# First-layer attention heads in pairs, and weights stored in runs of 4096 bytes

## The chip, the cores and the metric

The kernel runs on one core of a Trainium2 chip. The metric is the device time of one execution in microseconds, the median of several. The engines are called PE (matmul), PEld (PE's weight load), DVE (VectorE), ACT (ScalarE), POOL (GpSimd) and SP (SyncE, which issues nearly all DMAs here).

## The reference

Two blocks of two layers each work on 256 tokens of width 1024, in float32.

- The first block's layer, run twice: RMS norm with a modulation computed from a vector c; one projection into queries, keys and values of two attentions and two gates; attention A with 8 query heads on 2 key heads, a sliding window of 128 and a learned sink per head; attention B with 8 heads, which for 256 tokens is plain causal attention; two output projections, gated and added; `w_out`; then an MLP of width 4096 with squared ReLU.
- The second block: a pooling mixer and a mixture of 16 experts of width 256 (its layer 0, for 512 tokens: latent and context), then attention of 16 heads over latent and context and a second mixture of experts (its layer 1, 256 tokens). Each token goes to two experts of one group.

```
s = einsum('bnqhgd,bnkhd->bnhgqk', qb, kb) * HEAD_DIM ** -0.5     # masked, HEAD_DIM = 64
p = softmax(concatenate([s, sink], axis=-1), axis=-1)[..., :-1]   # attention A; B has no sink
hid = silu(h @ w_gate) * (h @ w_up) * gates;  y = hid @ w_down    # an expert
```

## The kernel before, in words

**Weights.** `plan` writes out one list of all weight pieces in the order in which they are used: pieces of 512 KB, 128 partitions by 1024 floats. `feed` has SP load the next piece of the list into a raw buffer as soon as one is free (7 raw buffers and, at stages, some pages of a shared pool). `pump` splits a piece into a high part H (a cast on ACT, L309) and a rest L (a subtraction on DVE, L310); `take` hands H and L to PE, which multiplies three times with them (L149 to L151). Between the weights stand pieces of the modulation matrices `w_ada` and `w_mod_2`, which DVE adds up (L353).

A weight matrix lies in memory as rows. A piece of `w_in`, `w_up`, `w_out`, `w_down`, `w_o_*` or `attn_wqkv_2` is 2 rows of 512 columns for each partition, so its DMA reads runs of 2048 bytes. A gate and up piece of an expert comes from two matrices with rows of 256 floats, so it takes two DMAs with runs of 1024 bytes. The pieces of `w_ada`, `w_mod_2` and of the experts' down matrix `moe_wd_2` already have runs of 4096 bytes.

**Order.** The program is written in Python in the order of the algorithm; a planner then orders the instructions of each engine by priority and by its own estimate of when each is ready, and gives out the buffers. An engine runs its list in that order and waits in place.

**Projection.** `block1` runs the first block's layer. Its in-projection has nine column blocks c; `proj` does a block in 8 parts (4 pieces times 2 token tiles), a part being 6 matmuls of 512 columns. After each part `fill` counts a tick and emits the work that `later` put down for that tick. The attention units are put down so: those of attention A after block 2, at ticks 2, 4, ..., 20, those of attention B after block 4, at ticks 2, 5, ..., 29.

**Attention units.** `attn_units` makes 10 units for 8 heads; unit i does S(i), T(i-1) and O(i-2).

- S (L917 to L938), one head: a matmul that puts the mask into a bank of PSUM, the scores of the first 128 queries against 128 keys and of the second 128 against 256, with contraction over 64 partitions (the even heads lie in partitions 0 to 63, the odd ones in 64 to 127); two maxima, the product with the scale, the minimum with the sink, two exponentials with their sums, the sink's exponential, the reciprocal, and two products with it.
- T (L945, L947): three transposes of 128x128 and a copy.
- O (L957 to L959): three products with the values, whose 64 result rows go to the lower or upper half of a bank; after the second head of a pair the result is split (L962, L963).

A float32 matmul is two instructions on PE, a transpose is one. `acc` gives one of 4 PSUM banks, `sm` (the probabilities) has 2 buffers, `pT` has 2.

**Experts.** In the second block's layer 0 an expert gathers 96 token rows from memory (POOL's indirect DMA, L1387), transposes and splits them (L1399 to L1402), multiplies (`gate_up`), takes silu (L1283), multiplies with the down matrix and adds the rows back to memory by an indirect DMA (L1440). In layer 1 the rows are gathered and scattered by matmuls. `attention2` (L1583 to L1616) already has its heads in pairs for O: the matmuls of two heads alternate between the lower and the upper 64 result rows. `dense_rest` runs only where an expert has over 96 tokens.

Of the kernel before, what the change touches and what calls it, by code (L numbers as in the profile page):

```python
# [12 lines left out]
F32 = mybir.dt.float32  # L13
# [5 lines left out]
AF = mybir.ActivationFunctionType  # L19
ALU = mybir.AluOpType  # L20
# [4 lines left out]
P = 128  # L25
# [58 lines left out]
class Kern:  # L84
# [75 lines left out]
    def plan(s):  # L160
# [14 lines left out]
        def kn(ap):  # L175
            return ap.rearrange("(k p) n -> p k n", p=P)
# [21 lines left out]
        def cols(key, src, c0, w0=512):  # L198
            for q in range(2):
                w(key + (q,), [(None, kn(src[q * 512:(q + 1) * 512, c0:c0 + w0]))], [P, 4, 512])  # L200

        def halves(key, src):
            for h in range(2):
                w(key + (h,), [(None, kn(src[:, h * 512:(h + 1) * 512]))], [P, 4, 512])

        s.rate = 0.0
        for l in range(2):
            if f"b1{l}" not in S:
                continue
            need(l, 1)  # L210
            s.rate = RATES[l][0]
            cols(("in", l, 0), A["w_in"][l], 0)
            w(("in", l, 1, 0), [(None, kn(A["w_in"][l][:, 512:768]))], [P, 8, 256])
            for i in range(7):
                cols(("in", l, 2 + i), A["w_in"][l], 768 + 512 * i)
            need(l, 2)
            halves(("oa", l), A["w_o_swa"][l])
            halves(("ob", l), A["w_o_moba"][l])
            for h in range(2):
                cols(("out", l, h), A["w_out"][l], 512 * h)  # L220
            need(l, 4)
            s.rate = RATES[l][1]
            for i in range(8):
                cols(("up", l, i), A["w_up"][l], 512 * i)
                if i == 6:
                    need(l, 5)
                if i:
                    halves(("dn", l, i - 1), A["w_down"][l][512 * (i - 1):512 * i])
            halves(("dn", l, 7), A["w_down"][l][512 * 7:])

        s.rate = 0.0

        def moe(l):
            for e in range(16):
                for q in range(2):
                    w(("gu", l, e, q),
                      [(0, kn(A["moe_wg_2"][l, e][q * 512:(q + 1) * 512])),
                       (1, kn(A["moe_wu_2"][l, e][q * 512:(q + 1) * 512]))], [P, 4, 512])
                if e:
                    w(("wd", l, e - 1), [(None, kn(A["moe_wd_2"][l, e - 1]))], [P, 2, 1024])  # L240
            w(("wd", l, 15), [(None, kn(A["moe_wd_2"][l, 15]))], [P, 2, 1024])
# [7 lines left out]
        if "l1" in S:  # L249
            need(3, 1)  # L250
            s.rate = RATES[2]
            for i in (2, 0, 1):
                s.rate = RATES[2] if i < 2 else 0
                cols(("qkv", i), A["attn_wqkv_2"][0], 512 * i)
            s.rate = 0.0
            need(3, 5)
            for i in range(2):
                halves(("wo", i), A["attn_wo_2"][0][512 * i:512 * (i + 1)])
            moe(1)
# [393 lines left out]
    def block1(s, l):  # L653
# [253 lines left out]
    def attn_units(s, l, br, qT, kT, v, oH, oL, qs):  # L907
        nc = s.nc
        pts, sms, ops = {}, {}, {}

        def S(h):
            b = (h % 2) * 64
            kp = (0 if (h // 4) == (h % 2) else 1) if br == 0 else 2 + h // 2
            q = qT[b:b + 64, 4 * br + h // 2]
            k = kT[b:b + 64, kp]
            ps = s.acc()
            nc.tensor.matmul(ps[:, 0:384], s.identb, s.maskb[br], start=True, stop=False, skip_group_check=True)  # L917
            nc.tensor.matmul(ps[:, 0:128], q[:, 0:128], k[:, 0:128], start=False, stop=False, skip_group_check=True)
            nc.tensor.matmul(ps[:, 128:384], q[:, 128:256], k, start=False, stop=True, skip_group_check=True)
            sm = s.bt([P, 384], tag="sm", bufs=2)  # L920
            mx = s.st([P, 2], tag="mx", bufs=4)
            nc.vector.tensor_reduce(mx[:, 0:1], ps[:, 0:128], AX.X, ALU.max, negate=True)
            nc.vector.tensor_reduce(mx[:, 1:2], ps[:, 128:384], AX.X, ALU.max, negate=True)
            nb = s.st([P, 2], tag="nb", bufs=4)
            nc.vector.tensor_mul(nb, mx, qs[:, :, h])
            if br == 0:
                nc.vector.tensor_scalar(nb, nb, s.nsink[:, l, h:h + 1], None, ALU.min)
            den = s.st([P, 2], tag="den", bufs=4)
            for t, c in ((0, slice(0, 128)), (1, slice(128, 384))):
                nc.scalar.activation(sm[:, c], ps[:, c], AF.Exp, bias=nb[:, t:t + 1], scale=qs[:, t, h:h + 1],  # L930
                                     accum_out=den[:, t:t + 1])
            if br == 0:
                es = s.st([P, 2], tag="es", bufs=4)
# [3 lines left out]
            for t, c in ((0, slice(0, 128)), (1, slice(128, 384))):  # L937
                nc.scalar.activation(sm[:, c], sm[:, c], AF.Copy, scale=den[:, t:t + 1])  # L938
            sms[h] = sm
# [10 lines left out]
        def O(h):  # L950
            b = (h % 2) * 64
            if h % 2 == 0:
                ops[h // 2] = s.acc()
            ps = ops[h // 2]
            p = pts.pop(h)
            c = (h // 4) * 64 if br == 0 else h * 64
# [3 lines left out]
            if h % 2:  # L960
                i = h // 2
                nc.scalar.copy(oH[:, i], ps[:, 0:256])  # L962
                nc.vector.tensor_sub(oL[:, i], ps[:, 0:256], oH[:, i].bitcast(F32))  # L963

        def unit(i):
            if i < 8:
                S(i)
            if 1 <= i < 9:
                T(i - 1)
            if i >= 2:  # L970
                O(i - 2)

        return [lambda i=i: unit(i) for i in range(10)]


# [248 lines left out]
    def dense_rest(s, l, fl, hD, ovg, Xs, rows, bank, hT, mo, wt):  # L1224
# [3 lines left out]
        with s.tc.If(v > 0):  # L1228
# [8 lines left out]
            for t, X in enumerate(Xs):  # L1237
# [7 lines left out]
                for e in range(16):  # L1245
                    ps = s.mm()
                    for j, nme in enumerate(("moe_wg_2", "moe_wu_2")):
                        for k in range(8):
                            if k % 2 == 0:
                                n += 1  # L1250
                                w = wt[n % 2].rearrange("p (k n) -> p k n", k=2)
                                nc.gpsimd.dma_start(w, A[nme][l, e][k * P:(k + 2) * P].rearrange("(k p) n -> p k n", p=P))
# [571 lines left out]
def tile_kernel(ctx, tc, A, out, dbg=None):  # L1824
    if True:
# [22 lines left out]
        "attn_qg_2", "attn_kg_2", "attn_wo_2", "moe_wrg_2", "moe_brg_2", "moe_wre_2", "moe_bre_2", "moe_wg_2",  # L1848
        "moe_wu_2", "moe_wd_2"]
# [18 lines left out]
```

## Time and profile before

| | us |
|---|---|
| median of 3 runs | 1464.56 (1464.15 to 1466.64) |
| profiled execution | 1466.67 |
| its span | 1464.4 |
| PE busy in the span | 1330.7 (91%) |
| DVE busy | 1187.1 (81%) |
| ACT busy | 907.4 (62%) |
| DMA moved | 362.22 MB, mean 247 GB/s |

PE's busy time counts modelled ends, and matmuls overlap: what a matmul costs is read from the start of one to the start of the next, not from its duration. The stages lie at these times of the span: the first block's layers from 38 and from 440 us, their attention units from 80 to 200 and from 490 to 592 us; the second block's layer 0 from 855 us, its experts from 945 to 1098 us; its layer 1 from 1123 us, its experts from 1304 to 1455 us.

### The profile page before, as it was taken

How to read it: one execution, taken by the hardware profiler on the slowest of the kernel's cores; microseconds unless marked ns; L12 is line 12 of the kernel's file. 1: busy time of each engine (PE TensorE's matmuls, PEld its weight loads, DVE VectorE, ACT ScalarE, POOL GpSimd, SP SyncE). 2: the span in 40 equal slices, each digit the busy share in tenths (PEclk: the TensorE clock that was granted, in tenths of full speed). 3: DMA queues.
4: the chain of work that ended last, by engine and by line, in shares of the span. 5: the costliest groups of instructions: out<-in, count | busy, mean ns of one | idle time of the engine just before them, and what ended most of it. 6: DMA issues, size and time to landing. Idle time of an engine off the chain costs nothing. (4 is left out here: it accounts for less than half of the span.)

```text
span 1464.4 us, 20599 instructions
## 1 busy us (share of the span) xinstructions
PE 1330.7 (91%) x7007; PEld 1050.7 (72%) x7007; DVE 1187.1 (81%) x1759; ACT 907.4 (62%) x1734; POOL 193.2 (13%) x183
## 2 busy tenths in 40 slices
PE   3899998999998999989999998599998879989898
PEld 2677776899886677767889887476665766776565
DVE  6896687776778888989999778598788798588687
ACT  2477745665656687467664635398784558557584
POOL 0330021000003300211001022322211220010000
PEclk9999999999999999989999999699999989989999
DMA  9676786888875566877888987699996533349981
GB/s 362 201 232 201 239 293 216 314 300 291 284 270 166 181 207 216 293 253 254 294 303 274 329 277 237 199 310 294 313 332 219 170 125 110 125 167 352 331 295 64
DMA packets 193336, 362.22 MB, mean 247 GB/s; under 512 B 20046, under 2 KB 91190, under 8 KB 193216
## 3 DMA queue, kind: packets, MB, share of 16 engines
q1 hardware_dynamic: 189024, 351.26, 71.2%
q0 software_dynamic: 3360, 7.91, 2.4%
q10 hardware_dynamic: 832, 1.57, 0.3%
q8 instruction: 59, 0.97, 0.3%
q14 instruction: 61, 0.50, 0.1%
HBM read 351.70 MB, written 12.88 MB: 249 GB/s over the span
## 5 line engine op out<-in xcount | busy, mean ns | idle before, releaser
L309 ACT CAST H<-raw 128x1024 fp32r<-128x1024 f32 x331 | 346.0, 1050 | 242.8 <-PE acc L151 92.2
L310 DVE TENSOR_TENSOR L<-raw,H 128x1024 fp32r<-128x1024 f32 x331 | 407.9, 1240 | 72.2 <-ACT H L309 70.1
L353 DVE SCALAR_TENSOR_TENSOR page<-raw,sc,page 128x1024 f32<-128x1024 f32 x218 | 282.0, 1301 | 24.0 <-DMA raw<-in_w_ada_dram 13.4
L149 PE MATMUL mm<-H,page 128*128 128x512 f32 (+1 forms) x416 | 167.4, 404 | 14.8 <-ACT page L581 10.5
L151 PE MATMUL mm<-H,page 128*128 128x512 f32 (+1 forms) x416 | 164.1, 396 | 1.4 <-DVE page L582 1.3
L150 PE MATMUL mm<-L,page 128*128 128x512 f32 (+1 forms) x416 | 164.0, 394 | 0.9 <-DVE L L310 0.8
L310 DVE TENSOR_TENSOR L<-page,H 128x1024 fp32r<-128x1024 f32 x104 | 125.2, 1221 | 31.8 <-ACT H L309 29.6
L149 PE MATMUL acc<-H,page 128*128 128x512 f32 x352 | 139.5, 396 | 0.0
L150 PE MATMUL acc<-L,page 128*128 128x512 f32 x352 | 139.4, 396 | 0.0
L151 PE MATMUL acc<-H,page 128*128 128x512 f32 x352 | 139.1, 395 | 0.0
L309 ACT CAST H<-page 128x1024 fp32r<-128x1024 f32 x104 | 108.2, 1052 | 42.2 <-PE mm L151 23.6
L809 PE MATMUL mm<-page,L 128*128 128x256 f32 x448 | 127.6, 285 | 0.0
L806 PE MATMUL mm<-page,H 128*128 128x256 f32 x448 | 127.5, 285 | 0.0
L808 PE MATMUL mm<-page,H 128*128 128x256 f32 x448 | 127.4, 284 | 0.0
L149 PE MATMUL mm<-H,gH 128*96 128x512 f32 x256 | 105.8, 413 | 11.4 <-PEq L1228 5.9
L149 PEld LDWEIGHTS mm<-H,page 128*128 128x128 f32 x416 | 80.2, 193 | 37.9 <-ACT page L581 12.9
L151 PE MATMUL mm<-H,gL 128*96 128x512 f32 x256 | 104.2, 407 | 1.9 <-DVE gL L1402 1.9
L150 PE MATMUL mm<-L,gH 128*96 128x512 f32 x256 | 103.4, 404 | 0.0
L151 PEld LDWEIGHTS mm<-H,page 128*128 128x128 f32 x416 | 80.3, 193 | 19.8 <-DVE page L582 4.3
L150 PEld LDWEIGHTS mm<-L,page 128*128 128x128 f32 x416 | 80.3, 193 | 17.4 <-issue 1.8
L806 PEld LDWEIGHTS mm<-page,H 128*128 128x128 f32 x448 | 85.8, 192 | 0.8
L808 PEld LDWEIGHTS mm<-page,H 128*128 128x128 f32 x448 | 85.8, 192 | 0.5
(380 smaller groups left out, 2573.6 us busy)
## 6 DMA issues: line engine op xcount, KB each, us to landing
raw<-in_w_mod_dram SPq DMA_DIRECT2D x94, 512.0 KB
raw<-in_w_ada_dram SPq DMA_DIRECT2D x92, 512.0 KB
raw<-in_w_in_dram SPq DMA_DIRECT2D x68, 512.0 KB
raw<-in_w_up_dram SPq DMA_DIRECT2D x61, 512.0 KB
raw<-in_w_down_dram SPq DMA_DIRECT2D x61, 512.0 KB
page<-in_moe_wd_dram SPq DMA_DIRECT2D x36, 512.0 KB
raw<-in_moe_wg_dram SPq DMA_DIRECT2D x64, 256.0 KB
raw<-in_moe_wu_dram SPq DMA_DIRECT2D x64, 256.0 KB
```

What stands on the lines that cost most here:

```text
L149: mm(ps, sH, wH, start=start, stop=False)
L150: mm(ps, sH, wL, start=False, stop=False)
L151: mm(ps, sL, wH, start=False, stop=stop)
L309: s.nc.scalar.copy(H, src)
L310: s.nc.vector.tensor_sub(Lo, src, H.bitcast(F32))
L353: nc.vector.scalar_tensor_tensor(a, raw, c, a, ALU.mult, ALU.add)
L806: nc.tensor.matmul(o, a, H[q // 2][:, 2 * (q % 2) + k], start=q == 0 and k == 0 and f % 2 == 0, stop=False, skip_group_check=True)
L808: nc.tensor.matmul(o, a, Lo[q // 2][:, 2 * (q % 2) + k], start=False, stop=False, skip_group_check=True)
L809: nc.tensor.matmul(o, b, H[q // 2][:, 2 * (q % 2) + k], start=False, stop=q == 3 and k == 1 and f % 2 == 1, skip_group_check=True)
```

## The change

**Heads in pairs.** A unit now belongs to two heads, and there are 6 of them for each attention. S(j) puts both masks into two banks, then alternates the heads' score matmuls (lower partitions, upper partitions), and does the small steps on statistics of two heads at once; the sink's exponential becomes an addition on DVE and one exponential for the pair. O(j) alternates the heads too, and takes 256 query columns at once for the first half of the keys. `pT` has 3 buffers. The units' ticks are 2, 6, ..., 22 and 2, 7, ..., 27.

**Weights in runs.** `_pack`, which runs on the host before the launch, stores `w_in`, `w_out`, `w_up`, `w_down`, `w_o_*`, `attn_wqkv_2`, `attn_wo_2` and the gate and up matrices (joined to `moe_gu`) piece by piece, each partition's 1024 floats together. So each of these pieces is one DMA with runs of 4096 bytes; the list's order, the pieces' contents and sizes in SBUF stay.

```diff
-        def w(key, parts, shape, rate=None):
+        def w(key, pieces, shape, rate=None):
             n = shape[1] // 2
             for h in range(2):
-                L.append(("w", key + (h,), [(i, src[:, h * n:(h + 1) * n]) for i, src in parts], [P, n, shape[2]]))
+                L.append(("w", key + (h,), [(None, pieces[h].rearrange("p (k n) -> p k n", k=n))], [P, n, shape[2]]))
...
-                for q in range(2):
-                    w(("gu", l, e, q),
-                      [(0, kn(A["moe_wg_2"][l, e][q * 512:(q + 1) * 512])),
-                       (1, kn(A["moe_wu_2"][l, e][q * 512:(q + 1) * 512]))], [P, 4, 512])
+                four(("gu", l, e), A["moe_gu"][l, e])
...
-                    s.later(u, 2 + 2 * i)
+                    s.later(u, 2 + 4 * i)
...
-                    s.later(u, 2 + 3 * i)
+                    s.later(u, 2 + 5 * i)
...
+        def S(j):
+            hs = (2 * j, 2 * j + 1)
+            pss = [s.acc(), s.acc()]
+            for ps in pss:
+                nc.tensor.matmul(ps[:, 0:384], s.identb, s.maskb[br], start=True, stop=False, skip_group_check=True)
...
+            for ps, (q, k) in zip(pss, qk):
+                nc.tensor.matmul(ps[:, 0:128], q[:, 0:128], k[:, 0:128], start=False, stop=False, skip_group_check=True)
+            for ps, (q, k) in zip(pss, qk):
+                nc.tensor.matmul(ps[:, 128:384], q[:, 128:256], k, start=False, stop=True, skip_group_check=True)
+            mx, nb, den = (s.st([P, 2, 2], tag=tag, bufs=4) for tag in ("mx", "nb", "den"))
...
+            nc.vector.tensor_mul(nb, mx, qs[:, :, 2 * j:2 * j + 2].rearrange("p t h -> p h t"))
             if br == 0:
-                nc.vector.tensor_scalar(nb, nb, s.nsink[:, l, h:h + 1], None, ALU.min)
+                nc.vector.tensor_tensor(nb, nb, s.nsink[:, l, 2 * j:2 * j + 2, None].to_broadcast([P, 2, 2]), ALU.min)
...
-                nc.scalar.activation(es, nb, AF.Exp, bias=s.sink[:, l, h:h + 1])
+                nc.vector.tensor_add(es, nb, s.sink[:, l, 2 * j:2 * j + 2, None].to_broadcast([P, 2, 2]))
+                nc.scalar.activation(es, es, AF.Exp)
...
-            p = s.bt([P, 384], tag="pT", bufs=2)
+            p = s.bt([P, 384], tag="pT", bufs=3)
...
-            nc.tensor.matmul(ps[b:b + 64, 0:128], v[:, 0, c:c + 64], p[:, 0:128], start=True, stop=True)
-            nc.tensor.matmul(ps[b:b + 64, 128:256], v[:, 0, c:c + 64], p[:, 128:256], start=True, stop=False)
-            nc.tensor.matmul(ps[b:b + 64, 128:256], v[:, 1, c:c + 64], p[:, 256:384], start=False, stop=True)
+            for b in range(2):
+                nc.tensor.matmul(ps[64 * b:64 * b + 64, 0:256], v[:, 0, c[b]:c[b] + 64], p[b][:, 0:256], start=True, stop=False,
+                                 skip_group_check=True)
+            for b in range(2):
+                nc.tensor.matmul(ps[64 * b:64 * b + 64, 128:256], v[:, 1, c[b]:c[b] + 64], p[b][:, 256:384], start=False, stop=True,
+                                 skip_group_check=True)
...
+        def unit(j):
+            if 1 <= j < 5:
+                T(2 * j - 2)
+            if j >= 2:
+                O(j - 2)
+            if 1 <= j < 5:
+                T(2 * j - 1)
+            if j < 4:
+                S(j)
```

## Rows read from the trace of the kernel before

**Rows 1.** The page, part 1: busy us of PE and PEld, share of the span, instructions.
```profile
PE 1330.7 (91%) x7007; PEld 1050.7 (72%) x7007; DVE 1187.1 (81%) x1759; ACT 907.4 (62%) x1734; POOL 193.2 (13%) x183
```

**Rows 2.** Windows: stretch, us, busy of each engine, PE's clock, DMA share, GB/s.
```profile
10.00:30.00 20.00, 4.16 (x18) 3.81 (x18) 15.64 (x14) 3.78 (x6) 1.66 (x2) 1.00 1.03 404
79.00:125.00 46.00, 45.57 (x226) 32.70 (x225) 39.89 (x84) 35.17 (x90) 13.29 (x12) 1.00 0.70 228
125.00:200.00 75.00, 75.00 (x361) 55.94 (x360) 52.60 (x97) 51.70 (x122) 0.00 (x0) 1.00 0.69 238
490.00:545.00 55.00, 52.48 (x262) 37.11 (x261) 47.73 (x92) 43.76 (x128) 7.73 (x6) 1.00 0.58 179
...
945.00:1008.00 63.00, 62.51 (x316) 45.16 (x315) 59.10 (x69) 57.17 (x82) 15.67 (x13) 1.00 1.01 301
1008.00:1080.00 72.00, 64.04 (x294) 43.97 (x293) 55.50 (x64) 52.34 (x77) 15.03 (x11) 0.93 1.01 311
1330.00:1380.00 50.00, 49.94 (x224) 35.19 (x223) 46.02 (x48) 40.14 (x50) 0.00 (x0) 1.00 1.04 349
```

**Rows 3.** Waits of PE, 79 to 200 us: total us, times, longest.
```profile
PE acc L945 <- ACT sm L938: 0.4, 1, 0.4
```

**Rows 4.** Timeline of PE in attention A's units: start us, us, instructions.
```profile
96.62 0.55 PE L945 MATMUL acc<-cst,sm 128*128 128x128 f32 x3
97.09 0.43 PE L957 MATMUL acc<-pT,va 128*64 128x128 f32 x2
...
97.89 0.34 PE L917 MATMUL acc<-maskb,identb 128*128 128x384 bf16 x1
98.16 0.49 PE L918 MATMUL acc<-kT,qT 64*128 64x128 f32 x2
98.48 0.59 PE L919 MATMUL acc<-kT,qT 64*128 64x256 f32 x2
99.01 0.44 PE L361 MATMUL tr<-cst,page 128*128 128x128 f32 x2
```

**Rows 5.** Timeline of PE in the second attention: start us, us, instructions.
```profile
1216.76 1.94 PE L1616 MATMUL mm<-pT,v 128*64 128x256 f32 x14
1218.63 0.33 PE L1601 MATMUL mm<-cst,q 128*128 128x128 f32 x1
```

**Rows 6.** Groups by line, the second attention's O: count, busy us, mean ns.
```profile
L1616 PE MATMUL mm<-pT,v 128*64 128x256 f32 x128 | 20.7, 389 | 0.0
```

**Rows 7.** Groups by line, the steps of S on DVE and ACT.
```profile
L930 ACT ACTIVATE sm<-acc,nb,qs 128x128 f32<-128x128 f32 x64 | 32.1, 507 | 4.1 <-DVE nb L925 2.1 <-DVE nb L927 2.0
L938 ACT ACTIVATE sm<-sm,den 128x128 f32<-128x128 f32 x64 | 25.7, 453 | 2.5 <-DVE den L936 2.5
...
L923 DVE TENSOR_REDUCE mx<-acc 128x1 f32<-128x256 f32 x32 | 13.2, 412 | 0.0
L930 ACT ACTIVATION_READ_ACCUMULATOR sm<-acc,nb,qs 128x1 f32 x64 | 12.7, 198 | 0.0
...
L922 DVE TENSOR_REDUCE mx<-acc 128x1 f32<-128x128 f32 x32 | 9.1, 286 | 11.7 <-PE acc L919 11.6
```

**Rows 8.** Timeline of ACT, layer 0's experts: start us, us, instructions.
```profile
971.97 0.38 ACT L1283 ACTIVATE hid<-mm 96x256 f32<-96x256 f32 x1 [0.33 <-PE mm L151]
...
1008.59 0.38 ACT L1283 ACTIVATE hid<-mm 96x256 f32<-96x256 f32 x1 [0.33 <-PE mm L151]
...
1078.05 0.38 ACT L1283 ACTIVATE hid<-mm 96x256 f32<-96x256 f32 x1 [0.32 <-PE mm L151]
```

**Rows 9.** Waits of ACT and PE, 1008 to 1090 us.
```profile
ACT H L309 <- DMA raw<-in_moe_wu_dram: 5.2, 8, 2.0
...
ACT H L309 <- DMA page<-in_moe_wu_dram: 3.1, 5, 2.0
...
PE mm L149 <- ACT gH L1401: 4.9, 3, 1.6
```

**Rows 10.** Waits of the whole span: ACT for pieces of `w_in`.
```profile
ACT H L309 <- DMA raw<-in_w_in_dram: 16.9, 15, 3.5
```

More of the change, by code (lines that the diff above doesn't have):

```diff
@@ L196, in need, with four @@
                 ada(*pend.popleft())
-        def cols(key, src, c0, w0=512):
+        def four(key, src):
             for q in range(2):
[L200 to L204, printed above, removed]
+                w(key + (q,), [src[2 * q], src[2 * q + 1]], [P, 4, 512])
         s.rate = 0.0
@@ L211, in plan @@
             s.rate = RATES[l][0]
-            cols(("in", l, 0), A["w_in"][l], 0)
-            w(("in", l, 1, 0), [(None, kn(A["w_in"][l][:, 512:768]))], [P, 8, 256])
+            four(("in", l, 0), A["w_in"][l])
+            w(("in", l, 1, 0), [A["w_in"][l][4], A["w_in"][l][5]], [P, 8, 256])
             for i in range(7):
-                cols(("in", l, 2 + i), A["w_in"][l], 768 + 512 * i)
+                four(("in", l, 2 + i), A["w_in"][l][6 + 4 * i:])
             need(l, 2)
-            halves(("oa", l), A["w_o_swa"][l])
-            halves(("ob", l), A["w_o_moba"][l])
+            four(("oa", l), A["w_o_swa"][l])
+            four(("ob", l), A["w_o_moba"][l])
             for h in range(2):
-                cols(("out", l, h), A["w_out"][l], 512 * h)
+                four(("out", l, h), A["w_out"][l][4 * h:])
             need(l, 4)
@@ L223, in plan @@
             for i in range(8):
-                cols(("up", l, i), A["w_up"][l], 512 * i)
+                four(("up", l, i), A["w_up"][l][4 * i:])
                 if i == 6:
@@ L227, in plan, with wd @@
                 if i:
-                    halves(("dn", l, i - 1), A["w_down"][l][512 * (i - 1):512 * i])
-            halves(("dn", l, 7), A["w_down"][l][512 * 7:])
+                    four(("dn", l, i - 1), A["w_down"][l][4 * (i - 1):])
+            four(("dn", l, 7), A["w_down"][l][28:])
         s.rate = 0.0
+        def wd(l, e):
+            w(("wd", l, e), [A["moe_wd_2"][l, e][k * P:(k + 1) * P] for k in range(2)], [P, 2, 1024])
         def moe(l):
             for e in range(16):
-                for q in range(2):
-                    w(("gu", l, e, q),
-                      [(0, kn(A["moe_wg_2"][l, e][q * 512:(q + 1) * 512])),
-                       (1, kn(A["moe_wu_2"][l, e][q * 512:(q + 1) * 512]))], [P, 4, 512])
+                four(("gu", l, e), A["moe_gu"][l, e])
                 if e:
-                    w(("wd", l, e - 1), [(None, kn(A["moe_wd_2"][l, e - 1]))], [P, 2, 1024])
-            w(("wd", l, 15), [(None, kn(A["moe_wd_2"][l, 15]))], [P, 2, 1024])
+                    wd(l, e - 1)
+            wd(l, 15)
         if "l0" in S:
@@ L253, in plan @@
                 s.rate = RATES[2] if i < 2 else 0
-                cols(("qkv", i), A["attn_wqkv_2"][0], 512 * i)
+                four(("qkv", i), A["attn_wqkv_2"][0][4 * i:])
             s.rate = 0.0
@@ L257, in plan @@
             for i in range(2):
-                halves(("wo", i), A["attn_wo_2"][0][512 * i:512 * (i + 1)])
+                four(("wo", i), A["attn_wo_2"][0][4 * i:])
             moe(1)
@@ L908, in attn_units @@
         nc = s.nc
[L909 to L925, printed above, removed]
-            if br == 0:
-                nc.vector.tensor_scalar(nb, nb, s.nsink[:, l, h:h + 1], None, ALU.min)
[L928 to L931, printed above, removed]
@@ L939, in S @@
-            sms[h] = sm
+            for i, h in enumerate(hs):
+                for t, c in ((0, slice(0, 128)), (1, slice(128, 384))):
+                    nc.scalar.activation(sms[h][:, c], sms[h][:, c], AF.Copy, scale=den[:, i, t:t + 1])
         def T(h):
@@ L1246, in dense_rest @@
                     ps = s.mm()
-                    for j, nme in enumerate(("moe_wg_2", "moe_wu_2")):
+                    for j in range(2):
                         for k in range(8):
@@ L1847, with _pack, cols, halves @@
         "c_ctx_2", "w_mod_2", "b_mod_2", "norm1_g_2", "norm2_g_2", "pool_w_2", "pool_b_2", "pool_ls_2", "attn_wqkv_2",
-        "attn_qg_2", "attn_kg_2", "attn_wo_2", "moe_wrg_2", "moe_brg_2", "moe_wre_2", "moe_bre_2", "moe_wg_2",
-        "moe_wu_2", "moe_wd_2"]
+        "attn_qg_2", "attn_kg_2", "attn_wo_2", "moe_wrg_2", "moe_brg_2", "moe_wre_2", "moe_bre_2", "moe_wd_2"]
+def _pack(inputs):
+    def cols(w, n=512):
+        lead, c = w.shape[:-2], w.shape[-1] // n
+        k = 1024 // n
+        w = w.reshape(-1, 8 // k, k, P, c, n).transpose(0, 4, 1, 3, 2, 5)
+        return w.reshape(*lead, c * 8 // k, P, 1024)
+    def halves(w):
+        lead, r = w.shape[:-2], w.shape[-2] // 512
+        w = w.reshape(-1, r, 2, 2, P, 2, 512).transpose(0, 1, 5, 2, 4, 3, 6)
+        return w.reshape(*lead, r * 4, P, 1024)
+    w = np.asarray(inputs["w_in"])
+    f = {"w_in": np.concatenate([cols(w[:, :, 0:512]), cols(w[:, :, 512:768], 256), cols(w[:, :, 768:])], axis=1)}
+    for n in ("w_out", "w_up", "attn_wqkv_2"):
+        f[n] = cols(np.asarray(inputs[n]))
+    for n in ("w_o_swa", "w_o_moba", "w_down", "attn_wo_2"):
+        f[n] = halves(np.asarray(inputs[n]))
+    f["moe_gu"] = cols(np.concatenate([np.asarray(inputs["moe_wg_2"]), np.asarray(inputs["moe_wu_2"])], axis=-1))
+    return {n: np.ascontiguousarray(a) for n, a in f.items()}
 def kernel(**inputs):
@@ L1858 @@
     feed = {n: np.ascontiguousarray(inputs[n]) for n in _INS}
+    feed.update(_pack(inputs))
     feed.update(_consts())
```

50 lines of the change are left out of this document (25 added, 25 removed).

## The prediction

> **What bounds the kernel now.** I read the page first, then windows by stage, then PE's timeline inside the stages that the change touches. PE is busy in 91% of the span and DVE in 81% [rows 1], but that is a mean over stages, and each part of the change lives in one stage.
>
> In the attention units of the first layers PE never stops: 45.57 of 46 us and 75.00 of 75 us in the first layer, 52.48 of 55 in the second [rows 2]. Its one wait there from 79 to 200 us is 0.4 us for a probability tile [rows 3]. The DMA engines are at 0.58 to 0.70, so loads do not limit these stretches; DVE is the next engine, 39.89 of 46 us in the first and 47.73 of 55 in the third [rows 2]. A microsecond taken off PE here is a microsecond of the span as long as DVE keeps up.
>
> In layer 0's experts the picture turns over halfway. ACT's silu (L1283) comes once for each expert, so its starts are the experts' period: 971.97 to 1008.59 us is four experts, 9.155 us each, with PE full; 1008.59 to 1078.05 is six experts, 11.58 us each [rows 8]. In the late stretch the DMA engines are at 1.01 while PE is busy for 64.04 of 72 us at a granted clock of 0.93, a mix of 2.4 GHz and of 1.2 GHz after stalls [rows 2]. ACT, which splits the weights, waits 5.2 and 3.1 us for up matrices, and PE then waits 4.9 us for the gathered rows that are queued on ACT behind those splits [rows 9]. At the pace of the early four, the six late experts would take 54.9 us instead of 69.5: 14.5 us are lost, and DMA is where they are lost. Layer 1's experts also have DMA at 1.04, yet PE is busy for 49.94 of 50 us [rows 2]: nothing to win there.
>
> **The heads in pairs.** From start to start [rows 4], one head now costs PE: transposes 97.09 - 96.62 = 0.47, O 97.89 - 97.09 = 0.80, mask 98.16 - 97.89 = 0.27, the scores of the first half 98.48 - 98.16 = 0.32, of the second 99.01 - 98.48 = 0.53. Sum 2.39 us, 4.78 for two heads. Two of these rows separate the matmul from the change of the array's shape. The first half is two instructions of 128 columns, the second half two of 256; with a for 128 columns and c for a change of shape, 2a + c = 0.32 and 4a + c = 0.53, so a = 0.105 and c = 0.11.
>
> After the change a pair has: two masks, 0.27 + 0.16 = 0.43; the first halves of two heads beside each other, 2a = 0.21; the second halves 4a + c = 0.53; two T, 0.94; O with four instructions of 256 and four of 128 columns, two and two beside each other, 4a + 2a + c = 0.74. Sum 2.85. Saved: 1.93 us a pair if everything that can run together does, of which 0.63 are S's instructions run beside each other, 0.63 O's, and the rest changes of shape that are made once for two heads. With 4 pairs, 2 attentions and 2 layers there are 16 pairs: 31 us.
>
> Can two heads run beside each other? For O the trace has a sister: in the second attention 14 recorded instructions of 256 columns (16 were issued) take 1218.63 - 1216.76 = 1.87 us [rows 5], where one behind the other they would take 16 x 0.21 = 3.4. So two column halves do run together. But over all 128 of them the busy time is 20.7 us [rows 6], between 27 one behind the other and 8 x 1.87 = 15 undisturbed: the planner puts other matmuls in between, and about half of the gain is realised. For S, where the heads lie in the lower and upper 64 partitions of the contraction, no two stand next to each other before, so no row shows it; it lies between nothing and its 0.63.
>
> The Trainium skill (TensorEngine Tiling (Array Packing), Key Properties) says that a change of tiling mode drains the engine, and that tiles work independently; the 0.11 above agrees with the first, rows 5 with the second for column halves, and for row halves no row here shows it. If row halves did not run together, the full sum would be 21 us instead of 31.
>
> I take 70% of the two savings by pairing (0.88), since S's instructions are one group that the planner now has little reason to split, and half of the shape changes (0.33): 1.2 us a pair, 19 us. From this I take off 2 us for DVE. Four pairs lie between 79 and 125 us; PE's 46 us become some 41, DVE has 39.9 less a few small steps [rows 2], so DVE is nearly as late as PE there. Term: -17 us; lower bound -3 (half of the shape changes in one layer alone), upper bound -31.
>
> ACT and DVE get little: each pair loses one product, one reciprocal and, in attention A, one minimum and one exponential, each shorter than the 286 ns of the smallest maximum [rows 7]. On neither engine is that the path; I count nothing.
>
> **The weights in runs.** The price of bytes comes from two saturated stretches [rows 2]. From 10 to 30 us only pieces with runs of 4096 bytes are loaded: 404 GB/s at a share of 1.03, 392 at full share. From 1330 to 1380 two thirds of the bytes are gate and up matrices with runs of 1024, one third down matrices with 4096: 349 at 1.04, or 336. An expert's three matrices, 3.15 MB, then take 9.4 us before and 8.0 after: 1.34 us less DMA time for each. In the late stretch alone this gives 6 x 1.34 = 8.0 us. The earlier experts save it too, and what SP has loaded ahead (7 raw buffers and 9 pages, 2.7 experts) then lasts longer: over 14 experts 18.8 us, more than the 14.5 that can be won. Gathers and scatters stay as they are. Term: -12, between -8 and -14.5. The gate and up piece also has one DMA instead of two on SP; SP is not late here, so nothing.
>
> The Trainium skill (DMA: Bandwidth & Descriptors, Specifications) puts full line rate at transfers of 512 B and more. By that rule runs of 1024 bytes lose nothing, and this term would be 0. The trace disagrees (336 against 392 GB/s), but these are different stages; I keep the rule as a rival.
>
> The runs of 2048 bytes lie in stretches where PE is full and DMA is at 0.7. ACT waits 16.9 us in 15 places for pieces of `w_in` [rows 10], most of it covered. Term: -1, between 0 and -3.
>
> Nothing else moves: the list of pieces keeps its order, so no queue gets a DMA earlier than another.
>
> **Sum.** -17 - 12 - 1 = -30 us on the profiled execution (span 1464.4, own time 1466.67, so 1436.7). The median of the runs is 2.1 us below that execution, so 1434.5.
>
> **Rivals.**
>
> 1. *The attention gain stops at the next engine.* DVE and ACT work in order, and what leaves PE comes back as waits for splits and probabilities. For: DVE at 39.89 of 46 and 47.73 of 55 us [rows 2]. Against: in 125 to 200 us DVE has 52.60 of 75, room for half of the pairs. Only 4 us of the 17 remain: 1464.6 - 4 - 12 - 1 = 1447.5.
> 2. *The runs' length does not matter.* What saturates the late experts is the number of bytes and the gathers beside them. For: 311 GB/s at 1.01 there, less than the 349 of layer 1 with the same runs [rows 2], so gathers take a part that stays. Against: the same two rates, 336 and 392. Then 1464.6 - 17 - 1 = 1446.5. The rule of the Trainium skill (DMA: Bandwidth & Descriptors, Specifications) would give this time.
> 3. *All of it.* Both halves run together everywhere and the experts keep PE's pace: 1464.6 - 31 - 14.5 - 3 = 1416.
> 4. *Slower: the ring of a pair is longer than its slot.* `sm` has two buffers, so the exponentials of the next pair wait for the transposes of this one, and these for one reciprocal over both heads. The ring, without any other work: four maxima 2 x (0.286 + 0.412) = 1.40, four exponentials with sums 4 x (0.507 + 0.198) = 2.82, four products 4 x 0.453 = 1.81 [rows 7], and at most 0.3 for each of two or three short steps: 6.8 us. Its slot in attention A: four parts of 6 matmuls of 0.23 us, 5.5, and a pair's own 2.9: 8.4 us. Before, one head had 3.8 in a slot of 2.8 + 2.4 = 5.2, so the ratio is the same, and PE waited 0.4 us [rows 3]; but splits and sums of 1 us stand between the steps, and a late pair holds two banks of PSUM instead of one. If each of the 16 pairs makes PE wait 1.9 us, the 30 are gone; at 2.5 us the time is 1464.6 - 30 + 40 = 1474.6.
> 5. *No change.* The planner orders by estimates, and those of DMAs and of statistics change everywhere; a new order could give back as much as is won: 1464.6.
>
> **How the numbers follow.** Forecast 0.62 (1434.5, its own range 1424 to 1445), rival 1: 0.15, rival 2: 0.06, rival 3: 0.08, rival 4: 0.06, rival 5: 0.03. The range of 8 in 10 is 1418 to 1451: it holds the forecast, rivals 1 and 2 and the edge of 3, and leaves out 4, 5 and the outer part of 3. About 0.2% (2.9 us) is what a measurement can tell from no change. Faster by more than that: 0.62 + 0.15 + 0.06 + 0.08 = 0.91; within it 0.03; slower 0.06.
>
> **What would show it.** In PE's timeline, the starts of two heads' L918-like instructions a few ns apart, and a pair at 2.9 to 3.6 us; PE still full from 79 us on, with attention B's last O some 8 us earlier in the first layer. If DVE waits vanish there and PE waits for probabilities, it was rival 1 or 4. In layer 0's experts, silu starts at 9.2 to 9.6 us apart through all of them and a DMA rate over 330 GB/s; periods of 11 us would be rival 2. Page part 3 should show a little over half the packets on SP's queue. The prediction is wrong if the attention units give less than 8 us over both layers, or the experts' stretch is not at least 8 us shorter.

## The result and the profile after

The changed kernel takes 1451.19 us (median of 4 runs, 1447.89 to 1451.84) against 1465.60 for the kernel before beside it: a ratio of 0.9894, 95% interval 0.9871 to 0.9918. It is 14.4 us faster. The forecast was 1434.5 with a range of 1418 to 1451: the sign was right, half of the 30 us is missing, and the time lies just outside the range.

The profiled execution took 1451.84 us, its span is 1450.0. Page, part 1 and the first line of part 3, of the changed kernel (answers to [rows 1]; part 3: packets, MB, share of 16 engines):

```profile
PE 1312.8 (91%) x6943; PEld 1036.2 (71%) x6943; DVE 1184.0 (82%) x1719; ACT 904.9 (62%) x1726; POOL 192.9 (13%) x183
...
q1 hardware_dynamic: 105456, 351.26, 70.1%
```

PE lost 17.9 us of busy time, and the span 14.4. Windows of the changed kernel, columns as in [rows 2]:

```profile
79.00:125.00 46.00, 40.08 (x186) 29.39 (x185) 38.02 (x67) 31.66 (x78) 15.05 (x12) 0.89 0.67 221
125.00:200.00 75.00, 74.69 (x374) 53.86 (x373) 52.93 (x95) 53.97 (x129) 0.00 (x0) 1.00 0.71 244
490.00:545.00 55.00, 48.93 (x236) 34.58 (x236) 48.62 (x75) 40.41 (x117) 8.30 (x6) 0.97 0.63 201
935.00:1000.00 65.00, 64.51 (x324) 46.55 (x323) 59.85 (x70) 58.49 (x84) 15.67 (x13) 1.00 0.97 321
1000.00:1080.00 80.00, 76.39 (x368) 53.54 (x367) 68.14 (x84) 65.55 (x97) 17.58 (x13) 0.96 0.96 324
```

In the first stretch PE was full before (45.57 of 46 us, clock 1.00). Now it is idle for 5.9 us and its granted clock falls to 0.89. In the experts the clock and PE's share are better than before, but not full.

To see where time goes, take the start of the same DVE instruction (the split of the same weight piece, L310 before, L304 after) in both traces: the difference is how far the changed kernel is behind (plus) or ahead (minus). The same for the other kernels below (us against before; the last three rows from the silu starts and the spans):

| | after | runs_only | pairs_only | head_stats | pairs_head |
|---|---|---|---|---|---|
| in the first layer's MLP (225.8 before) | +1.3 | -0.1 | -1.9 | -11.1 | -10.2 |
| after both layers (743.8 before) | -1.4 | +1.0 | -2.4 | -17.0 | -19.3 |
| first silu, layer 0's experts (947.5) | -7.3 | -1.6 | -8.2 | -21.3 | -23.1 |
| last silu (1097.5) | -14.0 | -9.4 | -6.8 | -29.1 | -21.3 |
| end of the span (1464.4) | -14.4 | -8.2 | -4.6 | -28.0 | -22.1 |

The table compares single executions. Two kernels below run the same code as the changed kernel (few_indirect) and as the kernel before (before_few) up to the experts: few_indirect stands at -3.6, -3.3 and -7.3 in the first three rows, before_few at +1.7, +1.3 and +0.2. So differences of about 2 us in a row tell nothing, and in the first row, where few_indirect was slowed less (see below), 5.

The attention units, which should have brought 17 us, had brought 1.4 by the end of both layers; the experts brought 6.7 instead of 12. Between the layers and the experts every kernel gained something, also runs_only, which has the old units. That stretch holds the pooling mixer, which the change does not touch; before's profile has a granted clock of 0.83 there (842 to 949.6 us), the changed kernel's 0.85 over the same work (840 to 942.1 us). I count this as no part of the mechanism.

**The pairs run beside each other.** PE's timeline of the changed kernel in attention A, columns as in [rows 4]:

```profile
96.10 0.33 PE L910 MATMUL acc<-maskb,identb 128*128 128x384 bf16 x1
96.35 0.49 PE L917 MATMUL acc<-kT,qT 64*128 64x128 f32 x4
96.68 0.60 PE L919 MATMUL acc<-kT,qT 64*128 64x256 f32 x4
...
140.18 0.60 PE L919 MATMUL acc<-kT,qT 64*128 64x256 f32 x4
140.71 0.65 PE L958 MATMUL acc<-pT,va 128*64 128x256 f32 x4
141.19 0.39 PE L961 MATMUL acc<-pT,va 128*64 128x128 f32 x4
```

Four score instructions of 128 columns, two heads, take 96.68 - 96.35 = 0.33 us; two of them, one head, took 0.32 before [rows 4]. Four of 256 take 140.71 - 140.18 = 0.53, as two did. So row halves do run beside each other, which no row had shown. The Trainium skill (TensorEngine Tiling (Array Packing), Key Properties) says that tiles work independently; for row halves the trace now agrees.

**What took it back.** Waits of the changed kernel, 79 to 200 us (us, times, longest; answers to [rows 3]):

```profile
PEld acc L947 <- ACT sm L941: 9.8, 12, 5.8
PE acc L947 <- ACT sm L941: 5.3, 1, 5.3
```

The transposes T wait for probabilities. The long wait lies between PE's instructions of 104.57 and 110.29 us. Here is what DVE, POOL, ACT and PE did then (timeline of the changed kernel; lines in order of engine):

```profile
97.09 0.69 DVE L619 TENSOR_TENSOR q<-mm,rstd 128x512 f32<-128x512 f32 x1 [1.88 <-POOL rstd L156]
...
98.83 1.77 DVE L630 TENSOR_TENSOR q<-q,SG 128x512 f32<-128x512 f32 x1
100.53 0.28 DVE L922 TENSOR_REDUCE mx<-acc 128x1 f32<-128x128 f32 x1
...
106.15 0.69 DVE L619 TENSOR_TENSOR q<-mm,rstd 128x512 f32<-128x512 f32 x1 [1.87 <-POOL rstd L156]
106.76 1.22 DVE L304 TENSOR_TENSOR L<-raw,H 128x1024 fp32r<-128x1024 f32 x1
107.89 1.22 DVE L937 TENSOR_TENSOR den<-den,es 128x4 f32<-128x4 f32 x1
109.04 0.68 DVE L630 TENSOR_TENSOR q<-q,SG 128x512 f32<-128x512 f32 x1
109.64 0.17 DVE L938 RECIPROCAL den<-den 128x4 f32<-128x4 f32 x1
...
104.47 1.64 POOL L156 TENSOR_TENSOR rstd<-rstd,nhalf 128x8 f32<-128x8 f32 x1
106.92 2.17 POOL L629 TENSOR_TENSOR q<-q,CG 128x512 f32<-128x512 f32 x1 [0.81 <-DVE q L619]
...
104.48 0.20 ACT L936 ACTIVATE es<-es 128x4 f32<-128x4 f32 x1
...
109.84 1.49 ACT L941 ACTIVATE sm<-sm,den 128x128 f32<-128x128 f32 x4 [3.25 <-DVE den L938]
...
104.57 0.39 PE L151 MATMUL mm<-H,page 128*128 128x512 f32 x1
110.29 0.48 PE L947 MATMUL acc<-cst,sm 128*128 128x128 f32 x1 [5.33 <-ACT sm L941]
```

The pair's exponentials are done at 104.7. Its sum and reciprocal (L937, L938) usually need 0.3 us of DVE, but in DVE's list they stand behind a normalisation step that waits for POOL (L619), a split, and a rotation step (L630): 109.6. The sum itself took 1.22 us here, beside POOL's L629, where its median is 0.16 (last section). The pair had met the same three steps once before: its scores began at 96.35 us, but its maxima (L922) stood behind an L619, a split and an L630 too, until 100.53. Both heads' products wait for that one reciprocal. PE stands still for 5.3 us, and its granted clock falls to 0.50, that is 1.2 GHz:

```profile
109.10:119.30 10.20, 9.01 (x32) 5.26 (x33) 6.17 (x14) 4.96 (x12) 0.00 (x0) 0.50 0.48 150
119.30:125.00 5.70, 5.70 (x27) 4.72 (x26) 5.50 (x9) 4.76 (x14) 0.00 (x0) 1.00 0.73 226
```

(windows of the changed kernel). Work of 9.0 busy us at half the clock costs an estimated 4.5 us more (half of 9.0): with the wait, some 10 us, all that the first layer's units had won. How long the clock stays low differs between executions. few_indirect below has the same units, and the same stop of 5.1 us before 109.28; its window:

```profile
109.30:112.70 3.40, 3.40 (x11) 1.50 (x11) 2.64 (x5) 1.78 (x6) 0.00 (x0) 0.50 0.60 182
```

So there the clock cost an estimated 1.7 us. In the second layer three waits of PE for probabilities, 1.0 to 1.6 us long (4.0 us together, 440 to 600 us), do part of the same. The experiments below test whether the joint statistics are the cause.

### The profile page after: what moved, and what is told of

It is laid out like the page before. It is cut to its first block, busy times and chain, and to the rows that moved or that the text cites. A ratio compares the mean times of both kernels' runs of the same rounds, so it can differ in the third digit from the quotient of the medians.

```text
span 1450.0 us, 20231 instructions
## 1 busy us (share of the span) xinstructions
PE 1312.8 (91%) x6943; PEld 1036.2 (71%) x6943; DVE 1184.0 (82%) x1719; ACT 904.9 (62%) x1726; POOL 192.9 (13%) x183
## 5 line engine op out<-in xcount | busy, mean ns | idle before, releaser
L304 DVE TENSOR_TENSOR L<-raw,H 128x1024 fp32r<-128x1024 f32 x331 | 410.0, 1247 | 70.0 <-ACT H L303 67.0
L347 DVE SCALAR_TENSOR_TENSOR page<-raw,sc,page 128x1024 f32<-128x1024 f32 x218 | 279.9, 1293 | 20.5 <-DMA raw<-in_w_ada_dram 11.8
L149 PE MATMUL mm<-H,page 128*128 128x512 f32 (+1 forms) x416 | 168.3, 407 | 15.3 <-ACT page L575 10.5
L304 DVE TENSOR_TENSOR L<-page,H 128x1024 fp32r<-128x1024 f32 x104 | 125.3, 1222 | 29.5 <-ACT H L303 27.8
```

The source lines that it names most:

```text
L149: mm(ps, sH, wH, start=start, stop=False)
L304: s.nc.vector.tensor_sub(Lo, src, H.bitcast(F32))
L347: nc.vector.scalar_tensor_tensor(a, raw, c, a, ALU.mult, ALU.add)
```

## The experiments

Four kernels split the result and its first cause, four more the theories, two the remainder. The kernel before beside them had medians of 1466.19, 1466.49 and 1464.87 us in the three groups.

**The runs alone** (runs_only): the weights in runs of 4096 bytes, the units of the kernel before. From the edit against the kernel before:

```diff
-        def w(key, parts, shape, rate=None):
+        def w(key, pieces, shape, rate=None):
...
+                four(("gu", l, e), A["moe_gu"][l, e])
```

> The weights in runs of 4096 bytes, the attention units single as in the kernel before. Theory: nearly all of the measured 14.4 us are the runs', since the pairs' gain on PE came back as waits: 1451 to 1455 us, the experts of layer 0 as after (their silu 9.15 us apart until the tenth, 8 us of delay in the last four instead of 14.5), and some 5 us ahead already before the experts. Rival (the pairs gave their 17 us after all, the runs nothing): 1465.

Measured: 1457.1 us (10 runs, 1454.68 to 1460.19), ratio 0.9934 [0.9915, 0.9954]: -9.1. This lies above the expected 1451 to 1455: the 6 us between the layers and the experts, which I had put to the runs, are not theirs (table, row 3). From first to last silu the experts take 142.2 us instead of 150.0.

**The pairs alone** (pairs_only): the changed units, weights as before. From the edit against the changed kernel; all other pieces go back in the same way:

```diff
-        def w(key, pieces, shape, rate=None):
+        def w(key, parts, shape, rate=None):
...
-                four(("gu", l, e), A["moe_gu"][l, e])
+                for q in range(2):
+                    w(("gu", l, e, q),
```

> The heads in pairs, the weights laid out as before. Theory: PE's time in the units falls by about 11 us a layer, and waits for probabilities and the clock's fall behind them take back 7 to 10 of it: 1460 to 1465 us. Rival (the pairs gave most): 1448 to 1452. If pairs and runs help each other, the two gains of this kernel and of the one with runs alone fall short of 14.4 us by more than 2.

Measured: 1461.45 us (10 runs), ratio 0.9959 [0.9933, 0.9985]: -4.7, as expected. The long wait is there (5.15 us, between PE's instructions of 103.69 and 109.23 us), and the sum of both parts, -13.8, is the whole, -14.4. Within the noise of these numbers (some 3 us each) the parts don't disturb each other; the missing time is missing in each.

**Small steps head by head** (head_stats): the changed kernel with matmuls in pairs, but maxima, sums and reciprocals for each head, inside the loop over the two heads.

```diff
-            mx, nb, den = (s.st([P, 2, 2], tag=tag, bufs=4) for tag in ("mx", "nb", "den"))
...
+                mx, nb, den = (s.st([P, 2], tag=tag, bufs=4) for tag in ("mx", "nb", "den"))
...
+                nc.vector.reciprocal(den, den)
...
-            nc.vector.reciprocal(den, den)
```

> As after, with the matmuls of S, T and O in pairs, but the small steps on the statistics and the reciprocal made for each head by itself, as in the kernel before. Theory (the first transposes wait for a reciprocal that waits for both heads' exponentials and stands behind other steps on DVE): the waits for probabilities fall to under 4 us, 1441 to 1446 us. Rival (the ring of two buffers, or DVE's load, which this kernel raises by some 6 us): no gain, 1449 to 1455.

**All of S early** (stat_first): the changed kernel, S put at a high priority in the planner's order.

```diff
         def S(j):
+            with s.tc.high_priority(offset=HP2):
+                S_(j)
+
+        def S_(j):
```

> As after, but all of S (masks, scores, maxima, exponentials, reciprocal, products) gets a higher priority in the planner, so that its steps on DVE and ACT are queued earlier against splits, sums and the rope's steps. Theory (the waits come from where the pair's steps stand in DVE's queue, behind splits and behind a step that waits for POOL): the waits of L947 for probabilities fall from 9.3 us to under 4, 1440 to 1446 us. Rival (two buffers of sm make a ring that is too long) and rival (DVE has no time left): within 3 us of the 1451 of after.

Measured: head_stats 1437.4 us (1432.74 to 1438.47), ratio 0.9783 [0.9735, 0.983]: -28.8. stat_first 1439.69 (1435.89 to 1441.94), ratio 0.9809 [0.976, 0.9858]: -26.5. Both gained a little more than expected. Waits of PE for probabilities, 79 to 600 us, of the changed kernel, of head_stats and of stat_first:

```profile
PEld acc L947 <- ACT sm L941: 17.8, 24, 5.8
PE acc L947 <- ACT sm L941: 9.4, 4, 5.3
```

```profile
PEld acc L944 <- ACT sm L937: 5.5, 12, 1.0
PE acc L944 <- ACT sm L937: 1.3, 3, 0.6
```

```profile
PEld acc L951 <- ACT sm L945: 8.0, 17, 1.3
PE acc L951 <- ACT sm L945: 1.7, 2, 0.9
```

The same matmuls, the same buffers, more small steps on DVE (head_stats) or the same ones earlier (stat_first): both give 12 to 14 us. So it was not DVE's load, but where the pair's steps stand in DVE's queue, measured against the transposes that need them (sm3 below tests the ring). Timeline of DVE in head_stats, the second pair of attention A, first maximum and last reciprocal:

```profile
94.33 0.29 DVE L923 TENSOR_REDUCE mx<-acc 128x1 f32<-128x128 f32 x1
...
100.74 0.16 DVE L935 RECIPROCAL den<-den 128x2 f32<-128x2 f32 x1
```

From this pair's first scores to its last reciprocal it takes 7.7 us (93.05 to 100.74) instead of 13.3 (96.35 to 109.64): the steps stand behind L619 and L630 once and not twice. stat_first leaves 11.8 us, with the reciprocal behind L619 and L630 as well, but begins them at 87.14 us, before PE needs the result. Window of head_stats, for the stretch that had stopped:

```profile
79.00:125.00 46.00, 42.65 (x218) 31.32 (x217) 42.46 (x88) 37.63 (x97) 14.23 (x11) 1.00 0.71 248
```

PE is again idle for 3.4 us, but in short pieces, and the clock stays at 1.00. DVE does more here than before the change (42.46 us against 39.89, [rows 2]).

**A longer ring** (sm3), with one buffer less for the transposes.

```diff
-                sm = s.bt([P, 384], tag="sm", bufs=2)
+                sm = s.bt([P, 384], tag="sm", bufs=3)
...
-            p = s.bt([P, 384], tag="pT", bufs=3)
+            p = s.bt([P, 384], tag="pT", bufs=2)
```

> The changed kernel with 3 buffers for the probabilities of a pair's heads instead of 2 (and 2 for their transposes instead of 3, for lack of room). My theory: PE's waits for probabilities (17.8 us on weight loads, 5.3 and 4.0 on matmuls) come from the place of the pair's sum and reciprocal in DVE's queue, behind splits and a step that waits for POOL; a further buffer moves neither. 1448 to 1454 us, waits within 3 us of the changed kernel's. Rival (the ring of a pair is too long for two buffers, my rival 4): the waits fall to the level before (some 3 us) and the time to 1436 to 1443.

Measured: 1453.41 us (1450.02 to 1457.38), ratio 0.9915 [0.9885, 0.9944]. PE's waits in sm3, 79 to 600 us:

```profile
PEld acc L947 <- ACT sm L941: 15.4, 24, 5.8
PE acc L947 <- ACT sm L941: 7.2, 3, 5.3
```

The long wait is untouched: the ring of my rival 4 is not what binds.

**The units later** (late_units).

```diff
-                    s.later(u, 2 + 4 * i)
+                    s.later(u, 6 + 4 * i)
```

> The changed kernel with attention A's units at ticks 6, 10, ..., 26 instead of 2, 6, ..., 22: the first pair's small steps meet other splits and sums in DVE's queue. Theory: the long wait of PE at 104 us in the first layer comes from the sums of modulation pieces and the wait for POOL that stand ahead of the pair's reciprocal; one part of the projection (5.5 us) later the pair meets them elsewhere, and the wait of 5.7 us falls under 3 us or goes: 1441 to 1449 us. Rival: the reciprocal over two heads is late wherever it stands: a wait of 4 to 6 us moves along with the unit, 1449 to 1453.

Measured: 1446.85 us (1443.75 to 1452.42), ratio 0.9877 [0.9844, 0.991]. PE's waits in late_units, 79 to 600 us:

```profile
PEld acc L947 <- ACT sm L941: 8.8, 23, 1.2
...
PE acc L671 <- DVE q L645: 7.5, 3, 3.6
...
PE acc L947 <- ACT sm L941: 0.8, 1, 0.8
```

The joint reciprocal is not late wherever it stands: four parts (some 5.5 us) later the longest wait is 1.2 us. But PE now waits for the steps that make the next queries (L671, three waits, the longest 3.6 us; in the changed kernel one of 0.8). In DVE's list only one maximum of 0.28 us stands between those steps and the rotation step before them, so why they are late is not shown. It is 8.6 us ahead after both layers, half of head_stats.

**Both repairs** (head_first): head_stats with S at high priority.

```diff
+            with s.tc.high_priority(offset=HP2):
+                S_(j)
```

> Both repairs at once: matmuls in pairs, small steps head by head, and all of S at high priority in the planner. Each alone gave 1437.4 and 1439.7. Theory: both take away the same wait, so together they give what the better one gives: 1434 to 1439 us, PE's waits for probabilities under 5.5 us on weight loads. Rival: the gains are of different waits and add up: 1424 to 1429. A second rival: a head's steps ahead of everything else delay the splits that PE needs for the projection: 1441 to 1448.

Measured: 1437.2 us (1435.71 to 1438.29), ratio 0.98 [0.978, 0.9821]. Waits for probabilities are gone (1.4 and 0.4 us), and the time is that of head_stats. It enters the experts 25 us ahead and leaves them 30 ahead, head_stats 21 and 29: most of what the layers win beyond head_stats is given back in the experts.

**The attention part with its repair** (pairs_head): the pairs of head_stats, weights as before. From the edit against the kernel before:

```diff
-        def S(h):
...
+        def S(j):
+            hs = (2 * j, 2 * j + 1)
+            pss = [s.acc(), s.acc()]
...
+                nc.vector.reciprocal(den, den)
```

> The kernel before with the matmuls of two heads in pairs and the small steps head by head, weights as before: the attention part of the change alone, without the joint statistics. Theory: this is the forecast's attention term; 15 to 20 us less than the kernel before, 1446 to 1451 us. Rival: the gain of 28.6 us seen with the weights in runs needs both parts (the faster units run into late pieces of weights otherwise): 1452 to 1458.

Measured: 1444.1 us (1442.59 to 1445.44), ratio 0.9855 [0.9816, 0.9894]: -20.8, a little more than I expected. After both layers it is 19.3 us ahead. This is the attention term as the forecast had meant it.

**Without gathers and scatters** (few_indirect from the changed kernel, before_few from the kernel before). Both leave out the gathers of layer 0's experts 3 to 15 and the scatters of experts 1 to 15.

```diff
+            if e < 3:
+                nc.gpsimd.indirect_dma_start(out=g, out_offset=None, in_=hD[:, :],
...
+            if e < 1:
+                nc.gpsimd.indirect_dma_start(out=mD[:, :], out_offset=bass.IndirectOffsetOnAxis(ap=idx[:, e:e + 1], axis=0),
```

> The changed kernel without the gathers of layer 0's experts 3 to 15 and without the scatters of experts 1 to 15 (these experts work on the rows of earlier ones, and their results are not added; the weights are loaded and multiplied as before). Theory: gathers and scatters take DMA time beside the weights (packets of 256 to 296 ns, a fifth of all packet time there), and that is why the late experts stay at 11 to 12 us: without them silu starts come every 9.15 us to the end, the experts' stretch is 5 to 7 us shorter, 1443 to 1447 us. Rival: the weights alone set the pace (8 DMAs in flight, raw buffers freed one after another by ACT and DVE): late experts stay at 11 to 12 us, 1448 to 1452.

> The kernel before (heads one by one, gate and up matrices in runs of 1024 bytes) without the gathers of layer 0's experts 3 to 15 and without the scatters of experts 1 to 15, as in the run before with the changed kernel, which then had all its silu 9.15 us apart and took 135.6 us from the first to the last instead of 143.3. Theory: gathers and scatters and the runs' length draw on the same DMA time; without gathers and scatters an expert's weights take 9.4 us in runs of 1024 bytes (336 GB/s), hardly more than PE's 9.15, and the lead of 2.7 experts covers the difference: first to last silu 136 to 140 us instead of 150.0, 1452 to 1457 us. Rival: short runs alone keep the late experts slow: 143 to 148 us from first to last, 1459 to 1464.

Measured: few_indirect 1443.72 us (1441.19 to 1446.46), ratio 0.9851 [0.9825, 0.9876]; before_few 1446.4 (1444.89 to 1448.63), ratio 0.9867 [0.9829, 0.9906], 6 us less than I expected. One line's instructions (count, shortest/median/longest ns, first and last start): silu in the changed kernel, in few_indirect and in before_few.

```profile
L1286 ACT ACTIVATE hid<-mm x16: 368/380/381, 940.2 to 1083.5; 96x256 f32<-96x256 f32 x16
```

```profile
L1286 ACT ACTIVATE hid<-mm x16: 379/380/381, 940.3 to 1075.8; 96x256 f32<-96x256 f32 x16
```

```profile
L1283 ACT ACTIVATE hid<-mm x16: 380/381/382, 947.7 to 1083.1; 96x256 f32<-96x256 f32 x16
```

First to last: 150.0 us before, 143.3 after, 135.5 and 135.4 without gathers and scatters, whatever the runs. Without them all periods are 9.15 to 9.17 us, PE's pace, but for the first two and the last. So in this stage the length of a run matters only together with gathers and scatters, which share the DMA engines with the weights. (The two kernels also lose the waits for gathered rows; these are not separated from the DMA time.) Part 3 of the page for single stretches (packets, MB, share): before 1008 to 1080 us, after 1000 to 1060, before_few 1000 to 1060, few_indirect 1000 to 1060.

```profile
q1 hardware_dynamic: 14937, 19.16, 80.1%
q0 software_dynamic: 1332, 3.16, 20.1%
```

```profile
q1 hardware_dynamic: 4575, 16.66, 77.0%
q0 software_dynamic: 1232, 2.90, 20.7%
```

```profile
q1 hardware_dynamic: 15402, 20.66, 101.6%
```

```profile
q1 hardware_dynamic: 5386, 19.57, 89.1%
```

Before, 19.16 MB took 0.801 x 72 = 57.7 us of all 16 engines, 332 GB/s; after, 16.66 MB took 46.2 us, 361 GB/s; in before_few short runs got 20.66 / 60.96 = 339, and in few_indirect long ones 19.57 / 53.46 = 366. So gathers and scatters take their own share, and change what a byte beside them costs by 1 to 2% only. An expert's 3.15 MB cost 9.47 us before and 8.72 after. The queue of gathers and scatters (q0) takes 20.1% of 72 us for six experts, 2.4 us each. So an expert needs 11.9 us of DMA before and some 11.1 after; PE needs 9.15.

## Why the forecast was half right

**Attention units, forecast -17, measured about -1 to -5.** By the prediction's own signs it is wrong in both parts: the units gave less than 8 us over both layers, and the experts' stretch is not 8 us shorter. The working on PE held. From start to start the units' lines take 38.9 us in the first layer and 39.7 in the second before, 32.8 and 31.8 after, the first with part of the slow clock in it. With the repair they take 28 in each, some 1.4 us less for each pair; the forecast took 1.2. pairs_head won 19.3 us by the end of both layers. Changed units alone won 2.4 there and 4.7 in the whole. So of the 22.7 us that the repaired units take off PE, 14.0 came in the changed kernel, and waits and the slow clock took most of these back.

The failed step is the sentence on DVE and ACT: "On neither engine is that the path; I count nothing." I counted durations and took 2 us off for DVE's load. The cost was not in load but in order: a reciprocal for two heads cannot start before the second head's last exponential, and by then DVE's list has other work in front of it, one piece of it waiting for POOL. The order cost 12 to 14 us: that much lies between the changed kernel and head_stats or stat_first, which split or move these steps and keep the matmuls. My rival 4 named that wait ("for one reciprocal over both heads") and the splits between the steps, but as a ring with two buffers and on the far side, slower than before; sm3 shows that a third buffer changes nothing. (Its sum also called the ratios of ring to slot the same; they are 3.8 to 5.2 and 6.8 to 8.4, 0.73 and 0.81.) Rival 1 had the size nearest (1447.5), with a reason that fell: DVE has 38.02 of 46 us, and head_stats, with more DVE work, is faster.

A second loss was not in the forecast at all: in the profiled execution the granted clock was 0.50 from inside the long stop on, for 10.2 us. In the kernel before, and in head_stats, the clock is 1.00 through this stretch.

The planner also put O's heads apart. Groups of four 256-column instructions beside each other (L958) were found in 3 of 16 pairs in the changed kernel, in 8 of 16 in head_stats (L955); in the others the second head's 256 columns only partly run beside the first head's 128 (starts of 102.18 and 102.19 us in head_stats). The forecast's 70% for pairing about held for S (10 of 16), not for O.

**Experts, forecast -12, measured -6.7 (after) and -7.8 (runs_only).** The mechanism was right: fewer packets, less DMA time, and the late experts move from 11.58 us [rows 8] to an average of 11.1 over the four from 1019.55 us to 1064.11:

```profile
1019.55 0.38 ACT L1286 ACTIVATE hid<-mm 96x256 f32<-96x256 f32 x1 [0.32 <-PE mm L151]
...
1064.11 0.38 ACT L1286 ACTIVATE hid<-mm 96x256 f32<-96x256 f32 x1 [0.33 <-PE mm L151]
```

(timeline of ACT, changed kernel). Slow periods begin at the tenth instead of the eighth. The term that was mis-sized is the DMA time of an expert: 1.34 us saved by forecast, 0.75 measured. The 392 GB/s came from 10 to 30 us, in another stage (where, besides, five of the pieces issued were `w_in`'s, with runs of 2048 bytes); in the experts runs of 4096 bytes got 361, and 366 without gathers and scatters. So these are not the reason for the difference, and no run here shows what is. The price of short runs (336 forecast, 332 measured) was right. From the 0.75, 14 experts save 10.5 us of DMA time, not 18.8, and 6.7 to 7.8 of them showed. Where the rest stays is open: the engines' share was 0.96 to 0.97 after, 1.01 before, so they were not always fed. The delay that is left in the changed kernel, 7.8 us, goes when gathers and scatters go.

Rival 2 (the length doesn't matter) fell: runs_only is 9.1 us faster than before, and in the same stage an expert's mix of 1024 and 4096 bytes stands at 332 GB/s, 4096 bytes alone at 361. The Trainium skill (DMA: Bandwidth & Descriptors, Specifications) puts full line rate at 512 bytes and more; by that rule runs_only would be level with before, and the trace disagrees.

**Runs of `w_in`, forecast -1:** runs_only is between -0.1 and +1.0 us in the layers, so nothing that can be told from noise.

**The place of the units, not in the sum:** it matters as well. A start 4 ticks later alone brings 5 to 7 us by the end of the layers (late_units at -8.6 against few_indirect's -3.3 and the changed kernel's -1.4); of the medians, 4.3 us apart, the ranges overlap. The list of pieces indeed kept its order and cost nothing.

With its repair the forecast would have come close, partly by luck: head_stats and head_first stand at 1437.4 and 1437.2, with -17 for the units, -7.8 for the experts instead of -12, and some 4 us from the stretch between them that nobody forecast and that the runs here don't explain.

## What to carry to other kernels

When two chains are joined to save small instructions, the first chain waits for the second, and the joined step goes to a new place in its engine's queue. Price that place (what stands ahead of it, and what that waits for), not the instruction's duration: here joined steps of some 0.3 us of DVE work cost 12 to 14 us, and splitting them again was free. A transfer's price is to be taken from the stage in which it will run: 4096-byte runs had 392 GB/s in one stage and 361 to 366 in another.

## What the runs showed of the hardware

- Around a stop of PE of 5.3 us the granted clock was 0.50 for 10.2 us, and PE was busy for 9.0 of them. After the same stop in few_indirect (5.1 us) it was 0.50 for 3.4 us. Short stops that add up to 3.4 us in 46 (head_stats) left it at 1.00. So in the two executions a microsecond of waiting in one piece cost an estimated 1.3 to 1.9 us, waiting and slow work together (6.8 us for 5.1, 9.8 for 5.3).
- The addition L937 on 128x4 elements took 1.22 us at 107.89 and 1.24 at 509.39, and 0.155 to 0.164 in its other 6 instances. Both long ones ran beside POOL's L629 (106.92 to 109.09 and 508.43 to 510.61) and ended 0.02 us after it. The Trainium skill (SBUF — State Buffer, SBUF: two separate sides) says that DVE and GpSimd share one pair of ports under an exclusive lock; these two cases agree with it, and no run here tests it alone.
